# Sparse attention: the two sums of an item's output moved from VectorE to GpSimd, with both halves copied out of PSUM by ScalarE

## The chip, the cores and the metric

The kernel runs on one core of a Trainium2 chip. The metric is the device time of one execution in microseconds. Engines are named as in the profile: PE is TensorE (PEld its weight loads), DVE is VectorE, ACT is ScalarE, POOL is GpSimd, SP issues most of the DMAs. Each engine works through its own list of instructions in order; an instruction that waits holds up all that stand behind it on that engine.

## The reference

Two decoder layers over 512 tokens of width 1024. Layer 0 mixes tokens with latent attention, layer 1 with sparse attention; each layer then cross-attends into 256 memory tokens and applies a SwiGLU block, and every sub-layer is followed by a LayerNorm of the scaled residual. The part that the change touches is the sparse attention of layer 1 (16 heads of 64 in 4 groups that share a key and value head, 128 selected keys for each query):

```python
def one_block(args):                      # 128 queries at a time
    ...
    dots = jnp.einsum('bqhd,bkd->bqhk', qi_blk, k_idx) * (IDX_DIM ** -0.5)
    score = jnp.einsum('bqh,bqhk->bqk', wi_blk, jax.nn.relu(dots))
    _, sel = lax.top_k(score, topk)       # topk = 128
    k_sel, v_sel = gather_rows(k, sel), gather_rows(v, sel)
    ...
    logits = jnp.einsum('bqngd,bqknd->bqngk', qg, k_sel) * (DSA_HEAD_DIM ** -0.5)
    logits = jnp.where(sel_ok[:, :, None, None, :], logits + bias, -jnp.inf)
    p = jax.nn.softmax(logits, axis=-1)
    o = jnp.einsum('bqngk,bqknd->bqngd', p, v_sel)
...
return from_blocks(out) @ w_o
```

## The kernel before, in words

Products of float32 accuracy are made from two parts: `split` (lines 97 to 100) rounds a tile to a high part on ACT (L98) and leaves the low part, the difference, to DVE or POOL (L100); `mm3` (L121 to L123) then adds three matmuls of such parts. `chunk` loads a block of weights and splits it; some blocks of the output projection of layer 1 (`wl`, 128x1024) are split on POOL.

The sparse attention does not gather. It keeps all keys and adds a mask, and it works in 16 items, number 4*qt + g for query block qt = 0 to 3 and group g = 0 to 3. An item has three steps. `dsa_scores` makes four score tiles (L1030 adds the mask, L1031 and L1032 the products), each in a PSUM bank of the tag "b"; DVE adds the bias and takes the row's extreme (L410), and ACT takes the exponential (L416). `dsa_t` transposes the weights of qt + 1 key blocks (L1045 for qt 0 and 1, L1047 for 2 and 3) into banks of the tag "a" and splits them (L98 on ACT, L100 on DVE; for qt 0 L103, L104, L105 on ACT and PE); it also takes the reciprocal of the row sums (L420, DVE) and spreads it over a tile `rb` (L421, POOL). `dsa_pv` multiplies by the values (L1057, L1058). The value weights hold high and low parts in 128 columns, so rows 0 to 63 and 64 to 127 of the result `po` have to be added: this is the "sum" of the change, in two instructions, since heads of even and odd number go to the lower and the upper half of `OF`. Then `rb` is transposed (L1068), `OF` is multiplied by it (L1069, DVE), and `OF` is split into the operands of the output projection, for items 0 to 11 on POOL (L1073, L1074), for items 12 to 15 on ACT and DVE (L98, L100, tiles 128x128).

There are four banks of the tag "a". They are handed out in turn to the transposes, to `po` and to the transposed `rb` (`pr_`); a bank can be written again when the last reader of the tile that was in it is done. Four more are of the tag "b".

A scheduler sets the order in which the instructions of different items stand on each engine. Items 0 to 11 are run with the scores and transposes of later items between their steps (`LA = 12`); from item 12 on, the scores are all out, and matmuls of the output projection of layer 1 (L121 to L123 with `wh`, `wl`) fill in between the items. Ahead of the stage, from about 840 to 890 us, DVE selects the top keys (L964, L965); behind it, from 980 us on, comes the rest of the output projection.

Of the kernel before, what the change touches and what calls it, by code (L numbers as in the profile page):

```python
# [15 lines left out]
ALU = mybir.AluOpType  # L16
# [4 lines left out]
P = 128  # L21
# [45 lines left out]
def tile_hybrid_mla_dsa_deepnorm_block(ctx: ExitStack, tc: tile.TileContext, A: dict, out: bass.AP):  # L67
    nc = tc.nc
# [9 lines left out]
    def nm(s):  # L78
        uid[0] += 1
        return f"{s}_{uid[0]}"  # L80

    def t2(dt=F32, shape=(P, 512)):
        return tp.tile(list(shape), dt, tag="t2", name=nm("t2"), bufs=39)
# [7 lines left out]
    def bank(tag, shape=(P, 512)):  # L91
        return pp.tile(list(shape), F32, tag=tag, name=nm("ps"))
# [4 lines left out]
    def split(h, l, src, eng=None, after=None):  # L97
        nc.scalar.copy(h, src)  # L98
        with behind(after):
            (eng or nc.vector).tensor_tensor(l, src, h.bitcast(F32), op=ALU.subtract)  # L100
# [423 lines left out]
    OF = {}  # L524
# [528 lines left out]
    def dsa_pv(qt, g, rb, PT):  # L1053
        ts_ = slice(P * qt, P * qt + P)
        po = bank("a")
        for kb in range(qt + 1):
            nc.tensor.matmul(po, VD[:, kb, g], PT[kb][0], start=(kb == 0), stop=False)  # L1057
            nc.tensor.matmul(po, VD[:, kb, g], PT[kb][1], start=False, stop=(kb == qt))  # L1058
        tmp = t2()
        nc.scalar.copy(tmp[0:64], po[64:128])  # L1060
        OF = t2(F32, (P, 2, P))
        ov = po[0:64].rearrange("p (i j q) -> p i j q", j=2, q=P)
        tv = tmp[0:64].rearrange("p (i j q) -> p i j q", j=2, q=P)
        for e in range(2):
            nc.vector.tensor_tensor(OF[64 * e:64 * e + 64], ov[:, :, e], tv[:, :, e], op=ALU.add)
        pr_ = bank("a", (P, 2, P))
        for i in range(2):
            nc.tensor.transpose(pr_[:, i], rb[:, 2 * i:2 * i + 2].rearrange("p a b -> p (a b)"), ident)  # L1068
        nc.vector.tensor_tensor(OF, OF, pr_, op=ALU.mult)  # L1069
        for i in range(2):  # L1070
            oh_, ol_ = OTd[2 * g + i]
            if qt < 3:
                nc.gpsimd.tensor_copy(oh_[:, ts_], OF[:, i])  # L1073
                nc.gpsimd.tensor_tensor(ol_[:, ts_], OF[:, i], oh_[:, ts_].bitcast(F32), op=ALU.subtract)  # L1074
            else:
                split(oh_[:, ts_], ol_[:, ts_], OF[:, i])
# [17 lines left out]
    for i in range(16):  # L1094
        a = 1 if i < LA else 0
        if i != LA:
            run_s(i + 1 + a)
            run_t(i + a)
        dsa_pv(*items[i], *PT.pop(i))
        for _ in range(NTI):  # L1100
            if todo:
                topk(*todo.pop(0))
# [94 lines left out]
```

## Time and profile before

| what | value |
|---|---|
| median of 3 runs | 1549.07 us (1548.76 to 1550.13) |
| the profiled execution's own time | 1550.88 us |
| its span in the profile | 1549.1 us |
| PE busy | 1510.6 us (98%) |
| DVE busy | 996.6 us (64%) |
| ACT busy | 650.1 us (42%) |
| POOL busy | 321.8 us (21%) |

The profiled execution took 1.8 us more than its span, and 1.8 us more than the median of the runs. The shares are means over the whole kernel; the stage that the change touches lies between about 890 and 985 us. A matmul's record is longer than the distance to the next one, so a busy PE is not PE at its peak.

### The profile page before, as it was taken

The page shows a single profiled execution, that of the slowest core. Times are in us where ns is not written, and L with a number is a line of the kernel's source. Part 1 is how long each engine was busy: PE and PEld are TensorE (multiplying, and loading weights), DVE is VectorE, ACT ScalarE, POOL GpSimd, SP SyncE. Part 2 cuts the span into 40 slices and gives each one's busy share as a digit, 9 for nine tenths or more (in the row PEclk, how much of TensorE's full clock was granted, in tenths as well). Part 3 has the DMA queues.
Part 4 walks back from the last instruction along what each step waited for, and adds up shares of the span by engine and source line. Part 5 has one row for each costly group of instructions (what it writes and reads, how often), then busy time and mean ns, then how long its engine had stood idle before and what let it go on. Part 6 is the DMA issues. An engine that isn't in the chain of part 4 may idle for free.

```text
span 1549.1 us, 20803 instructions
## 1 busy us (share of the span) xinstructions
PE 1510.6 (98%) x7940; PEld 1290.5 (83%) x7940; DVE 996.6 (64%) x1709; ACT 650.1 (42%) x1150; POOL 321.8 (21%) x332
## 2 busy tenths in 40 slices
PE   9999999999999999999999899999999999999997
PEld 8788888988888888888888688898988888888886
DVE  6888868554746565654668979675548465656535
ACT  4677743343233333332246478334332333333320
POOL 2322101000132331400124553010002322324003
PEclk9999999999999999999999999999999999999999
DMA  6234424322323232223242337333323232322321
GB/s 221 71 99 110 147 82 139 120 87 91 130 88 116 75 121 86 98 90 109 83 150 69 96 109 245 109 109 110 109 90 128 78 113 94 106 94 88 96 94 55
DMA packets 51321, 166.79 MB, mean 108 GB/s; under 512 B 5300, under 2 KB 11748, under 8 KB 49172
## 3 DMA queue, kind: packets, MB, share of 16 engines
q1 hardware_dynamic: 50788, 164.41, 31.7%
q8 instruction: 62, 1.02, 0.3%
q10 hardware_dynamic: 432, 1.05, 0.2%
q14 instruction: 39, 0.32, 0.1%
HBM read 161.20 MB, written 9.47 MB: 110 GB/s over the span
## 4 chain that ended last, share of the span: by engine, by line
PE 80%; DVE 10%; ACT 3%; DMA 3%; issue 2%; POOL 1%; POOLq 0%; ACTq 0%; DVEq 0%; SPq 0%
PE ps L121 25%; PE ps L123 25%; PE ps L122 25%; DVE t L100 2%; DVE t L965 2%; DVE m L964 1%; ACT wh L98 1%; DVE wl L100 1%; ACT t L98 1%; PE ps L329 1%; PE ps L1047 1%; PE ps L1045 1%; POOL sm L272 1%; PE ps L1030 1%; ACT t L416 1%
## 5 line engine op out<-in xcount | busy, mean ns | idle before, releaser
L121 PE MATMUL ps<-t,wh 128*128 128x512 f32 (+1 forms) x1264 | 459.2, 363 | 3.4 <-DVE t L100 3.4
L122 PE MATMUL ps<-t,wh 128*128 128x512 f32 (+1 forms) x1264 | 458.1, 362 | 1.4 <-DVE t L100 1.4
L123 PE MATMUL ps<-t,wl 128*128 128x512 f32 (+1 forms) x1264 | 458.1, 362 | 0.0
L98 ACT CAST wh<-raw 128x1024 fp32r<-128x1024 f32 (+2 forms) x218 | 227.4, 1044 | 455.2 <-PE ps L122 168.2
L100 DVE TENSOR_TENSOR wl<-raw,wh 128x1024 fp32r<-128x1024 f32 (+2 forms) x197 | 253.2, 1287 | 226.7 <-ACT wh L98 224.9
L121 PE MATMUL ps<-wh,t 128*128 128x512 f32 (+2 forms) x838 | 305.0, 364 | 2.6 <-DVE t L100 1.5
L123 PE MATMUL ps<-wh,t 128*128 128x512 f32 (+2 forms) x838 | 303.1, 362 | 0.0
L122 PE MATMUL ps<-wl,t 128*128 128x512 f32 (+2 forms) x838 | 302.3, 361 | 0.0
L121 PEld LDWEIGHTS ps<-t,wh 128*128 128x128 f32 x1264 | 238.6, 189 | 41.8 <-DVE t L100 5.5
L122 PEld LDWEIGHTS ps<-t,wh 128*128 128x128 f32 x1264 | 238.6, 189 | 38.1 <-DVE t L100 1.9
L123 PEld LDWEIGHTS ps<-t,wl 128*128 128x128 f32 x1264 | 238.6, 189 | 37.2
L121 PEld LDWEIGHTS ps<-wh,t 128*128 128x128 f32 x838 | 159.0, 190 | 26.1 <-DVE t L100 1.7
L123 PEld LDWEIGHTS ps<-wh,t 128*128 128x128 f32 x838 | 158.9, 190 | 24.0 <-DVE t L100 0.5
L98 ACT CAST t<-ps 128x512 fp32r<-128x512 f32 (+2 forms) x249 | 122.9, 525 | 133.0 <-PE ps L329 87.8
L122 PEld LDWEIGHTS ps<-wl,t 128*128 128x128 f32 x838 | 159.1, 190 | 23.0
L270 POOL TENSOR_SCALAR sm<-sm 128x1 f32<-128x1 f32 x32 | 19.0, 594 | 674.7 <-DVE sm L304 634.5
L100 DVE TENSOR_TENSOR t<-ps,t 128x512 fp32r<-128x512 f32 (+2 forms) x249 | 144.1, 606 | 22.3 <-ACT t L98 20.7
L98 ACT CAST wh<-t 128x1024 fp32r<-128x1024 f32 x56 | 58.9, 1052 | 141.5 <-PE ps L122 123.5
L100 DVE TENSOR_TENSOR wl<-t,wh 128x1024 fp32r<-128x1024 f32 x56 | 71.2, 1272 | 64.8 <-ACT wh L98 63.1
L843 DVE TENSOR_TENSOR t<-ps,t 128x512 f32<-128x512 f32 x44 | 30.4, 692 | 120.4 <-PE ps L123 120.4
L100 DVE TENSOR_TENSOR t<-t,t 128x512 fp32r<-128x512 f32 (+2 forms) x113 | 83.9, 746 | 23.7 <-ACT t L98 21.5
L98 ACT CAST t<-t 128x512 fp32r<-128x512 f32 (+2 forms) x113 | 64.5, 574 | 57.7 <-POOL t L777 33.3
(177 smaller groups left out, 1690.5 us busy)
## 6 DMA issues: line engine op xcount, KB each, us to landing
raw<-in_ffn_in_dram SPq DMA_DIRECT2D x88, 512.0 KB, 3.2
t<-in_ffn_dg_dram SPq DMA_DIRECT2D x16, 1024.0 KB, 5.0
raw<-in_xa_k_dram SPq DMA_DIRECT2D x16, 512.0 KB, 3.2
raw<-in_xa_v_dram SPq DMA_DIRECT2D x16, 512.0 KB, 3.7
raw<-in_xa_q_dram SPq DMA_DIRECT2D x16, 512.0 KB, 3.7
raw<-in_xa_o_dram SPq DMA_DIRECT2D x16, 512.0 KB, 3.2
raw<-in_ffn_dl_dram SPq DMA_DIRECT2D x12, 512.0 KB, 3.2
scr<-vscr SPq DMA_DIRECT2D x16, 319.5 KB, 4.4
```

The source lines that it names most:

```text
L98: nc.scalar.copy(h, src)
L100: (eng or nc.vector).tensor_tensor(l, src, h.bitcast(F32), op=ALU.subtract)
L121: nc.tensor.matmul(ps, st[0], mv[0], start=start, stop=False, skip_group_check=more)
L122: nc.tensor.matmul(ps, st[0], mv[1], start=False, stop=False, skip_group_check=more)
L123: nc.tensor.matmul(ps, st[1], mv[0], start=False, stop=stop, skip_group_check=more)
L270: nc.gpsimd.tensor_scalar(a, var, scale, eps, op0=ALU.mult, op1=ALU.add)
L272: nc.gpsimd.tensor_tensor(b, a, mhalf, op=ALU.pow)
L329: nc.tensor.transpose(pt[:, k], x_of(tt)[:, 512 * n + P * k:512 * n + P * k + P], ident)
L416: nc.scalar.activation(Sx, src, AF.Exp, bias=nb, scale=scale, accum_out=self.sm[:, i:i + 1])
L843: nc.vector.tensor_tensor(sg, pu, sg, op=ALU.mult)
L964: nc.vector.max(out=m8, in_=acc[:, :n])
L965: nc.vector.match_replace(out=acc[:, :n], in_to_replace=m8, in_values=acc[:, :n], imm_value=-3e38)
```

## The change

The second half of `po` is no longer read by DVE straight from PSUM. ACT copies both halves of `po` to SBUF (two copies in place of one), and the two sums are made on POOL from these copies. All else of the step stays: the transposes of `rb`, the multiplication on DVE, the splits. An item uses one 128x512 buffer of the tag "t2" more.

```diff
@@ dsa_pv
-        tmp = t2()
-        nc.scalar.copy(tmp[0:64], po[64:128])
+        halves = []
+        for rows in (slice(64, 128), slice(0, 64)):
+            tmp = t2()
+            nc.scalar.copy(tmp[0:64], po[rows])
+            halves.append(tmp[0:64].rearrange("p (i j q) -> p i j q", j=2, q=P))
         OF = t2(F32, (P, 2, P))
-        ov = po[0:64].rearrange("p (i j q) -> p i j q", j=2, q=P)
-        tv = tmp[0:64].rearrange("p (i j q) -> p i j q", j=2, q=P)
         for e in range(2):
-            nc.vector.tensor_tensor(OF[64 * e:64 * e + 64], ov[:, :, e], tv[:, :, e], op=ALU.add)
+            nc.gpsimd.tensor_tensor(OF[64 * e:64 * e + 64], halves[1][:, :, e], halves[0][:, :, e], op=ALU.add)
```

In the changed kernel the copy is line 1062, the sum 1066, and each later line of `dsa_pv` has a number higher by one (the multiplication is L1070, the splits on POOL L1074 and L1075). The scheduler orders the whole stage anew. Three places of the lists follow.

First place: DVE, where the selection of the keys ends (L969) and the results of items 0 and 1 meet the scores of item 4 (L410). Before:

```order
L969 TENSOR_SCALAR t_1536_10860<-t_1462_10553 128x512
L1065 TENSOR_TENSOR t_1691_11517<-ps_11512,t_1690_11515 64x256 x2
L1069 TENSOR_TENSOR t_1691_11517<-t_1691_11517,ps_11520 128x256
L1065 TENSOR_TENSOR t_1707_11576<-ps_11571,t_1706_11574 64x256 x2
L1069 TENSOR_TENSOR t_1707_11576<-t_1707_11576,ps_11579 128x256
L410 ISA t_1710_11590,sm_11592<-ps_11594,t_1710_11590 128x256
```

The same place on DVE of the changed kernel:

```order
L969 TENSOR_SCALAR t_1536_10860<-t_1462_10553 128x512
L1070 TENSOR_TENSOR t_1692_11519<-t_1692_11519,ps_11522 128x256
L1070 TENSOR_TENSOR t_1709_11580<-t_1709_11580,ps_11583 128x256
L410 ISA t_1712_11594,sm_11596<-ps_11598,t_1712_11594 128x256
L410 ISA sm_11596 128x1
```

The four sums are gone; both multiplications, of items 0 and 1, still stand ahead of item 4's first L410.

Second place: POOL around the result of item 4 (`t_1764` is its `OF` before, `t_1769` in the changed kernel; `t_1783` and `t_1789` are item 5's). Before:

```order
L421 COPY t_1754_11749<-sm_11750 128x256
L100 TENSOR_TENSOR wl_12669<-raw_12666,wh_12668 128x1024
L421 COPY t_1773_11817<-sm_11818 128x256
L1073 CAST t_1665_11459<-t_1764_11778 128x128 x2
L1074 TENSOR_TENSOR t_1665_11459<-t_1764_11778,t_1665_11459 128x128 x2
L1073 CAST t_1666_11460<-t_1783_11846 128x128
```

The same place on POOL of the changed kernel:

```order
L421 COPY t_1758_11757<-sm_11758 128x256
L100 TENSOR_TENSOR wl_12701<-raw_12698,wh_12700 128x1024
L1066 TENSOR_TENSOR t_1769_11788<-t_1768_11786,t_1767_11784 64x256 x2
L421 COPY t_1778_11827<-sm_11828 128x256
L1074 CAST t_1665_11459<-t_1769_11788 128x128 x2
L1075 TENSOR_TENSOR t_1665_11459<-t_1769_11788,t_1665_11459 128x128 x2
L1066 TENSOR_TENSOR t_1789_11858<-t_1788_11856,t_1787_11854 64x256 x2
L421 COPY t_1798_11897<-sm_11898 128x256
L100 TENSOR_TENSOR wl_12731<-raw_12728,wh_12730 128x1024
```

Item 4's sums stand behind a split of weights (`wl`, 128x1024); a second such split stands between the sums of items 5 and 6, and a third, further on, between those of 7 and 8.

Third place: PE between the last product of item 13 and the first of item 14 (`ps_12417` and `ps_12443` are item 13's `po`; `ps_12507` and `ps_12535` item 14's; L1047 are item 14's transposes; L121 to L123 with `wh`, `wl` belong to the output projection). Before:

```order
L1058 MATMUL ps_12417<-t_1941_12414,t_1449_10402 128x512
L1047 MATMUL ps_12471<-ident,t_1921_12349 128x128 x3
L1047 MATMUL ps_12480<-ident,t_1921_12349 128x128 x4
L123 MATMUL ps_12604<-wh_12608,t_1665_11459 128x512
L121 MATMUL ps_12605<-wh_12608,t_1665_11459 128x512
L122 MATMUL ps_12605<-wl_12609,t_1665_11459 128x512
L123 MATMUL ps_12605<-wh_12608,t_1665_11459 128x512
L1047 MATMUL ps_12489<-ident,t_1921_12349 128x128 x4
L1047 MATMUL ps_12498<-ident,t_1921_12349 128x128 x4
L121 MATMUL ps_12602<-wh_12608,t_1665_11459 128x512
L1057 MATMUL ps_12507<-t_1956_12476,t_1449_10402 128x512
```

The same place on PE of the changed kernel:

```order
L1058 MATMUL ps_12443<-t_1954_12440,t_1449_10402 128x512
L1047 MATMUL ps_12499<-ident,t_1934_12375 128x128 x2
L1047 MATMUL ps_12508<-ident,t_1934_12375 128x128 x4
L123 MATMUL ps_12636<-wh_12640,t_1665_11459 128x512
L121 MATMUL ps_12637<-wh_12640,t_1665_11459 128x512
L1047 MATMUL ps_12517<-ident,t_1934_12375 128x128 x4
L122 MATMUL ps_12637<-wl_12641,t_1665_11459 128x512
L123 MATMUL ps_12637<-wh_12640,t_1665_11459 128x512
L121 MATMUL ps_12634<-wh_12640,t_1665_11459 128x512
L1047 MATMUL ps_12526<-ident,t_1934_12375 128x128 x4
L122 MATMUL ps_12634<-wl_12641,t_1665_11459 128x512
L1057 MATMUL ps_12535<-t_1970_12504,t_1449_10402 128x512
```

There are six matmuls of the output projection here instead of five, and one transpose of item 14 less; the last group of transposes has moved behind five of them.

## Rows read from the trace of the kernel before

**Rows 1.** The page, part 1: the span, and PE's busy time.
```profile
span 1549.1 us, 20803 instructions
PE 1510.6 (98%) x7940; PEld 1290.5 (83%) x7940; DVE 996.6 (64%) x1709; ACT 650.1 (42%) x1150; POOL 321.8 (21%) x332
```
**Rows 2.** Windows: stretch, length, busy us (count) of PE, PEld, DVE, ACT, POOL; clock; DMA.
```profile
905.00:915.00 10.00, 8.97 (x65) 7.99 (x66) 6.90 (x34) 8.86 (x29) 5.90 (x11) 1.00 0.19 55
...
985.00:1000.00 15.00, 15.00 (x68) 12.43 (x67) 10.53 (x15) 5.24 (x7) 0.00 (x0) 1.00 0.47 143
```
**Rows 3.** Waits, 880 to 985 us: waiter, releaser, total us, times, longest.
```profile
PE ps L1030 <- DVE sm L410: 7.8, 2, 7.4
DVE t L1065 <- ACT t L1060: 6.8, 8, 1.9
PE ps L1068 <- DVE t L1065: 1.2, 2, 0.9
...
PE ps L1068 <- DVE t L100: 0.2, 1, 0.2
```
**Rows 4.** Groups by line and shape, 880 to 985 us: busy us, mean ns.
```profile
L1065 DVE TENSOR_TENSOR t<-ps,t 64x256 f32<-64x256 f32 x32 | 13.3, 416 | 7.4 <-ACT t L1060 6.8 <-POOL wl L100 0.4
L100 POOL TENSOR_TENSOR wl<-raw,wh 128x1024 fp32r<-128x1024 f32 x5 | 12.0, 2391 | 0.0
L1074 POOL TENSOR_TENSOR t<-t,t 128x128 fp32r<-128x128 f32 x24 | 10.7, 459 | 0.5
L1060 ACT COPY t<-ps 64x512 f32<-64x512 f32 x16 | 9.3, 583 | 6.5 <-PE ps L1058 6.3
```
**Rows 5.** Lines 776 and 778 on POOL: ns min/median/max, first and last start.
```profile
L776 POOL TENSOR_TENSOR t<-t,t x16: 737/740/857, 445.0 to 1422.8; 128x256 f32<-128x256 f32 x16
L778 POOL TENSOR_TENSOR t<-t x16: 1184/1720/1728, 445.7 to 1423.5; 128x256 f32<-128x256 f32 x16
```
**Rows 6.** Timeline, items 1 and 4: start, us, engine, line, [idle before <-releaser].
```profile
903.49 0.58 ACT L1060 COPY t<-ps 64x512 f32<-64x512 f32 x1
...
904.16 0.85 DVE L1065 TENSOR_TENSOR t<-ps,t 64x256 f32<-64x256 f32 x2 [1.86 <-ACT t L1060]
905.12 0.42 DVE L1069 TENSOR_TENSOR t<-t,ps 128x256 f32<-128x256 f32 x1
...
905.45 0.42 DVE L410 CUSTOM_DVE_ANT_0 t<-ps,t 128x256 f32<-128x256 f32 x1
...
905.93 0.38 PE L1030 MATMUL ps<-t,identr 128*128 128x256 f32 x1 [0.37 <-DVE sm L410]
```
**Rows 7.** Timeline, item 4: the weight split on POOL, and item 5's first product.
```profile
919.51 2.38 POOL L100 TENSOR_TENSOR wl<-raw,wh 128x1024 fp32r<-128x1024 f32 x1
...
921.81 0.47 PE L1057 MATMUL ps<-t,t 128*128 128x512 f32 x1
```
**Rows 8.** Timeline, from item 13's last product to item 14's first.
```profile
967.62 0.48 PE L1058 MATMUL ps<-t,t 128*128 128x512 f32 x1
...
968.13 0.58 ACT L1060 COPY t<-ps 64x512 f32<-64x512 f32 x1 [1.27 <-PE ps L1058]
...
968.62 0.72 ACT L416 ACTIVATE t<-t,sm 128x512 f32<-128x512 f32 x1
...
968.75 0.85 DVE L1065 TENSOR_TENSOR t<-ps,t 64x256 f32<-64x256 f32 x2 [0.94 <-ACT t L1060]
...
969.15 0.39 PE L122 MATMUL ps<-wl,t 128*128 128x512 f32 x1
...
969.38 0.40 PE L123 MATMUL ps<-wh,t 128*128 128x512 f32 x1
...
969.72 0.39 DVE L1069 TENSOR_TENSOR t<-t,ps 128x256 f32<-128x256 f32 x1
...
970.07 1.29 DVE L100 TENSOR_TENSOR t<-ps,t 128x512 fp32r<-128x512 f32 x2
...
970.89 0.43 PE L1057 MATMUL ps<-t,t 128*128 128x512 f32 x1
```

## The prediction, made before the changed kernel had run

> **What bounds the kernel now.** I read the page first: PE is busy 1510.6 us of a span of 1549.1 us [rows 1]. The change lies in one stage of some 95 us, so I went to the windows of that stage. From 905 to 915 us PE is at 8.97 of 10 us, ACT at 8.86, DVE at 6.90 and POOL at 5.90; from 985 us on PE runs without a gap, 15.00 of 15 us, while DVE, ACT and POOL have room [rows 2]. So the stage ends when PE has worked off its list, and only what makes PE wait counts.
>
> The view of the waits says what that is. DVE stands 6.8 us in all at the sums that the change takes from it (L1065), each time because ACT's copy is late. PE itself waits little: 7.8 us at L1030 for DVE, of which one wait of 7.4 us is at the end of the key selection, ahead of the first sum; then 1.2 us and 0.2 us at L1068 [rows 3]. What a relieved DVE could still give PE is thus 7.8 - 7.4 + 1.2 + 0.2 = 1.8 us. That is the ceiling of the gain, although DVE loses 32 sums and 13.3 us of work [rows 4].
>
> **The change part by part.** DVE loses two sums of 0.416 us per item, 0.85 us as a pair [rows 4, 8]. ACT gains a copy of 0.583 us per item, 16 in all [rows 4]. A copy lets the next instruction on ACT start 0.49 us after its own start (968.13 to 968.62) [rows 8], so two copies take 0.49 + 0.58 = 1.07 us from the first start to the last end.
>
> POOL gains 32 sums. No row shows a 64x256 sum on POOL. The nearest are sums of the same 256 columns over 128 partitions: 0.740 us at the median of L776, 1.720 us at that of L778 [rows 5]; the lower end is the 0.459 us of a 128x128 difference, half the columns [rows 4]. I take 0.74 us, since L776 also reads two tiles that other engines have left long ago, while L778 shares its time with DVE's splits of SBUF tiles. A pair then takes 0.70 + 0.74 = 1.44 us, the second starting a little before the first ends, as the pair of DVE does (0.85 for two of 0.416). The two ends make a pair of 0.9 or of 3.4 us.
>
> The rule that speaks against the change: the Trainium skill's GPSIMD Engine Reference (section "Engine selection") sends an elementwise sum to VectorE, because GpSimd is about twice as slow with two inputs. Here the trace agrees: 0.740 us of L776 against DVE's 0.416 us for the same columns is a factor of 1.8. By the page's factor of two the pair would be an estimated 1.66 us and the sum below about 1 us larger.
>
> So from the first copy to the multiplication it takes 1.07 + 1.44 and two handovers of 0.05 = 2.61 us; before, 968.13 to 969.72 = 1.59 us [rows 8]. The chain of each item grows by 1.0 us. DVE now waits for POOL at the multiplication instead of for ACT at the sums, and behind that wait stand scores and splits for PE. Whether it costs anything depends on the place.
>
> *First place, items 0 and 1: +1.4 us.* In DVE's list both multiplications stand ahead of item 4's first L410, and PE's next score (L1030, 905.93) waits for that L410 (905.45) to free its bank [rows 6]. ACT's second copy for item 0 pushes item 1's copy from 903.49 to some 903.94 (0 to 0.49 us are possible; I take 0.45, as ACT's splits between the two are bound to one another). Then 1.07 of copies, 0.05, 1.44 of sums, 0.05 and the multiplication, 0.33 us ahead of L410 (905.12 to 905.45): 903.94 + 2.94 = 906.88 instead of 905.45. POOL is free in time: item 0's sums end near 902.9, and its four splits, at most 4 x 0.459 = 1.8 us [rows 4], near 905. Nothing covers this, since PE has no other row there. With sums of 0.46 us it would be +0.9, with 1.72 us +3.4.
>
> *Second place, items 4 and 6: +1.2 us.* A weight split of 2.391 us [rows 4] stands on POOL ahead of item 4's sums, where before it ran from 919.51 beside the work of the other engines and delayed only a spreading [rows 7]. Item 4's multiplication, a score and the splits of item 6's transposes on DVE, and item 5's transpose of `rb` on PE, now wait for it. Each of the two places costs between nothing (the split is over when the copies are) and 2.4 us; before, DVE and PE moved on at 921.81 [rows 7], just when that split ended, so it can be late only by little: I take 0.6 us each. The same split ahead of item 8's sums has more distance, and I put it at nothing; without that distance it costs as much as the others.
>
> *Third place, from item 12 to 13, 13 to 14 and 14 to 15: +3.0 us.* Here the chain is closed. Item 13's last product starts at 967.62; the copy follows at 968.13, the multiplication at 969.72, DVE's split of item 14's first transposes at 970.07, and item 14's first product at 970.89 [rows 8]. PE has 5 matmuls of the output projection and the transposes to fill that time, and they fill it to the tenth. In the changed kernel the chain is 1.0 us longer, and the filler is six matmuls for five but one transpose less; besides, its last transposes need the bank that the multiplication frees. A matmul is 0.23 us (969.15 to 969.38) [rows 8], so 0.8 to 1.0 us stay uncovered. The step from 14 to 15 is alike. From 12 to 13 there are six more matmuls than before (1.4 us), but item 12's sums stand on POOL behind those of item 11 and its four splits (1.44 and up to 1.8 us), and the transposes of item 13 wait for their multiplication; I take 1.2 us, between 0 and 2.9. In all 1.2 + 1.0 + 0.8 = 3.0.
>
> *The other items: -0.6 us.* For items 2, 3, 5 and 7 to 11 scores and transposes of later items stand between a product and whatever needs its bank, three us and more of PE's list; the longer chain fits in, and DVE has 0.85 us less to do per item. If this cover were gone they would cost up to 1.0 us each, 8 us. Of the ceiling of 1.8 us I take a third. Item 15's result is needed some 18 groups of three projection matmuls after its last product, 18 x 3 x 0.23 = 12 us, and costs nothing.
>
> Sum: 1.4 + 1.2 + 3.0 - 0.6 = +5.0 us. The profiled execution would go from 1550.88 to 1555.9 us; since it lies 1.8 us above the median of the runs shown, I add the difference to the median: 1549.07 + 5.0 = 1554.1 us.
>
> **The rivals.** *The relief of DVE wins.* If the scheduler's new order hides every longer chain, PE gets back the 1.8 us that it still waits for DVE: 1547.3 us, not slower. For it: DVE is near its limit in much of the stage and stood 6.8 us at L1065 [rows 3]. It decides where the sums on POOL end before DVE reaches the multiplication; at items 0 and 1 that would need a pair of sums in less than zero time, so it can only hold later on.
>
> *The waits fall where PE has other work.* The first place stays (+1.4), the third is half covered by the reordered filler (+1.5), the rest cancels: +2 to +3 us, 1551.1 to 1552.1 us. For it: the scheduler has put more matmuls of the projection between items 12 and 13. Against it: from 13 to 14 the filler is the same.
>
> *POOL is slowed by DVE.* If the sums take 1.72 us like L778 [rows 5], the pair is 2.0 us longer: 2.0 more at the first place and at each of three handovers, 4 more in the middle, 12 on top of 5.0: +17, 1566 us; with only the three handovers hit, where DVE splits the SBUF tiles of items 12 to 15, 5.0 + 6 = +11, 1560 us. The Trainium skill's page SBUF — State Buffer ("Who interferes with whom") names this: a DVE instruction with two SBUF inputs and a GpSimd instruction that reads SBUF lock each other out. The trace's L778 bears it out elsewhere; in this stage nearly all of DVE's work has one input in PSUM (t<-ps,t), as L1065 has [rows 4], which speaks against it here.
>
> **How the numbers follow.** My forecast (+3.1 to +8 us) 0.58; POOL slowed or the covered items uncovered (+8 and more) 0.14; waits covered (+0.5 to +3.1) 0.20; relief wins 0.08. A measurement of this kernel can tell about 0.2%, 3.1 us, from no change. Slower by more than that: 0.58 + 0.14 = 0.72; faster by that much is beyond the ceiling of 1.8 us and would need PE's waits to be undercounted: 0.05; the rest, 0.23, is no change. The range leaves out the relief case and the upper half of the slowed one: from +0.5 to +11 us, 1549.6 to 1560.0.
>
> **What would show it.** First step: in the changed trace DVE waits for POOL at L1070 near 905 us, and PE's L1030 behind it comes near 907.4 instead of 905.93; an L1030 at 906 would refute it. POOL's sums: a median near 0.74 us. Second: a wait at L1070 for item 4 that ends with a POOL row behind `wl`. Third: from item 13's last product to item 14's first about 4.2 us instead of 3.27. DVE's waits for ACT at the sums gone, those for POOL at L1070 larger than 6.8 us in all. Wrong I would be if DVE's list reaches L1070 late enough that POOL is done, or if POOL holds buffers that ACT and DVE want back, a wait that I have not priced.

## The result: 13 us slower, and the profile after

The changed kernel takes 1561.96 us (median of 6 runs, 1559.99 to 1563.31), the kernel before 1548.98 us (6 runs beside it). The ratio is 1.0079, with a 95% interval from 1.0068 to 1.0089: slower by 13.0 us, 0.8%. The direction is the one foretold; the size is not: +5.0 us was forecast, and 1562 us lies beyond the range. The profiled execution of the changed kernel took 1559.99 us.

On the page PE is as busy as before [rows 1], and the span is longer: what is new is idle time of PE.

```profile
span 1558.2 us, 20828 instructions
PE 1510.3 (97%) x7940; PEld 1288.8 (83%) x7940; DVE 984.7 (63%) x1677; ACT 657.3 (42%) x1166; POOL 345.1 (22%) x364
```

Windows between the same pieces of work show where (columns as in [rows 2]). They run from item 0's first product to item 4's, on to item 12's, and on to the first transposes of the next norm (L329). First before, then the changed kernel:

```profile
897.01:917.02 20.01, 17.93 (x126) 15.50 (x125) 14.50 (x57) 17.07 (x52) 9.98 (x17) 1.00 0.17 54
917.02:958.46 41.44, 40.97 (x241) 34.43 (x240) 37.97 (x111) 36.32 (x90) 21.00 (x43) 1.00 0.75 257
958.46:1006.93 48.47, 48.35 (x240) 39.68 (x239) 35.25 (x72) 21.15 (x45) 4.25 (x9) 1.00 0.39 128
```

```profile
895.71:918.48 22.77, 17.75 (x127) 15.40 (x125) 12.21 (x54) 18.01 (x55) 15.06 (x24) 1.00 0.15 48
918.48:964.73 46.25, 41.75 (x245) 34.42 (x243) 33.02 (x96) 41.80 (x105) 31.89 (x58) 1.00 0.67 231
964.73:1016.72 51.99, 48.46 (x238) 38.88 (x236) 30.07 (x57) 22.18 (x44) 11.09 (x19) 1.00 0.35 119
```

PE's idle time (length less PE's busy time) goes from 2.1 to 5.0 us, from 0.5 to 4.5 and from 0.1 to 3.5: 2.9, 4.0 and 3.4 us more, 10.4 in all. The granted clock is 1.00 in all six stretches.

The waits from 880 to 1000 us (waiter, releaser, total us, times, longest) answer to [rows 3]. L1070 is the multiplication that was L1069, L1066 the sums, L1062 the copies, L1069 now the transpose of `rb`.

```profile
DVE t L1070 <- POOL t L1066: 29.4, 16, 4.4
...
PE ps L1030 <- DVE sm L410: 9.4, 2, 7.4
...
PE ps L1047 <- DVE t L1070: 3.9, 5, 1.4
...
PE ps L1069 <- DVE t L1070: 2.3, 2, 1.5
...
PE ps L1057 <- DVE t L1070: 1.7, 2, 0.9
...
PE ps L1045 <- DVE t L1070: 1.4, 1, 1.4
```

DVE waits for POOL at all 16 multiplications, 29.4 us, where it waited 6.8 us for ACT before. That alone costs nothing. The last four rows do: PE waits 3.9 + 2.3 + 1.7 + 1.4 = 9.3 us for the multiplication itself, a releaser that [rows 3] does not have at all. The transposes L1047, L1045 and L1069 and the product L1057 write into PSUM banks that are handed out in turn. The only thing that they need of the multiplication is such a bank, one that still holds `pr_`, the transposed factor that the multiplication has yet to read. At L1030 another 9.4 - 7.4 = 2.0 us stand for DVE's queue, where before it was 0.4.

The groups by line and shape show that the operations cost what was expected of them:

```profile
L1066 POOL TENSOR_TENSOR t<-t,t 64x256 f32<-64x256 f32 x32 | 23.2, 725 | 36.7 <-ACT t L1062 35.5
L1062 ACT COPY t<-ps 64x512 f32<-64x512 f32 x32 | 18.6, 581 | 6.2 <-PE ps L1058 4.3 <-POOL t L1075 1.3
```

A sum on POOL takes 725 ns (0.74 us was taken from L776), 1.74 times DVE's 416.

**The first place.** The timeline of items 0 and 1 (start, us, engine, line, idle time and releaser):

```profile
901.82 0.42 DVE L1070 TENSOR_TENSOR t<-t,ps 128x256 f32<-128x256 f32 x1 [2.03 <-POOL t L1066]
...
902.30 0.71 PE L1045 MATMUL ps<-ident,t 128*128 128x128 f32 x4 [1.43 <-DVE t L1070]
...
902.77 0.48 PE L104 MATMUL ps<-t,identn 128*128 128x512 f32 x1
...
903.28 0.58 ACT L105 CAST t<-ps 128x512 fp32r<-128x512 f32 x1 [1.83 <-PE ps L104]
903.89 1.17 ACT L1062 COPY t<-ps 64x512 f32<-64x512 f32 x2
...
905.14 1.51 POOL L1066 TENSOR_TENSOR t<-t,t 64x256 f32<-64x256 f32 x2 [1.40 <-ACT t L1062]
...
906.68 0.42 DVE L1070 TENSOR_TENSOR t<-t,ps 128x256 f32<-128x256 f32 x1 [4.43 <-POOL t L1066]
907.02 0.42 DVE L410 CUSTOM_DVE_ANT_0 t<-ps,t 128x256 f32<-128x256 f32 x1
...
907.50 0.39 PE L1030 MATMUL ps<-t,identr 128*128 128x256 f32 x1 [1.93 <-DVE sm L410]
```

Read it downwards, as one chain. Item 0's multiplication comes late; the transposes L1045 wait 1.43 us for its bank; ACT's split L105 waits for them; item 1's two copies stand behind that split in ACT's queue; then come the sums, item 1's multiplication, L410 and, at 907.50, PE's next score. In this execution the stage had begun 1.30 us earlier than in the profile of before (first product of item 0 at 895.71 against 897.01), so the 1.57 us from 905.93 [rows 6] to 907.50 are a loss of 1.57 + 1.30 = 2.9 us.

**The second place.** Around item 4, POOL, DVE and PE:

```profile
921.72 2.35 POOL L100 TENSOR_TENSOR wl<-raw,wh 128x1024 fp32r<-128x1024 f32 x1
922.00 1.19 ACT L1062 COPY t<-ps 64x512 f32<-64x512 f32 x2
...
924.04 1.52 POOL L1066 TENSOR_TENSOR t<-t,t 64x256 f32<-64x256 f32 x2
...
925.60 0.42 DVE L1070 TENSOR_TENSOR t<-t,ps 128x256 f32<-128x256 f32 x1 [1.05 <-POOL t L1066]
...
926.16 0.41 PE L1069 MATMUL ps<-ident,t 128*128 128x128 f32 x2 [1.48 <-DVE t L1070]
```

The copies end at 923.19, the sums start only at 924.04 when the weight split is done, and item 5's transpose of `rb` waits 1.48 us.

Further on, at item 8, the third such split (941.67 to 944.07) pushes back more than the sums. It pushes the splits of item 7's result on POOL (L1074, L1075), and item 8's second copy on ACT waits for those:

```profile
945.42 0.58 ACT L1062 COPY t<-ps 64x512 f32<-64x512 f32 x1 [1.31 <-POOL t L1075]
...
946.05 0.66 PE L1047 MATMUL ps<-ident,t 128*128 128x128 f32 x4 [0.56 <-ACT t L1062]
...
948.11 0.50 PE L1057 MATMUL ps<-t,t 128*128 128x512 f32 x1 [0.94 <-DVE t L1070]
```

A copy takes nothing from POOL but the buffer of the tag "t2" that it writes to, so this is a wait for a buffer that POOL held. PE waits 0.56 + 0.94 = 1.50 us there.

**The third place.** From item 13's last product to item 14's first, which answers to [rows 8]:

```profile
975.34 0.48 PE L1058 MATMUL ps<-t,t 128*128 128x512 f32 x1
...
975.86 1.19 ACT L1062 COPY t<-ps 64x512 f32<-64x512 f32 x2 [1.80 <-PE ps L1058]
...
977.12 1.53 POOL L1066 TENSOR_TENSOR t<-t,t 64x256 f32<-64x256 f32 x2 [5.96 <-ACT t L1062]
...
978.69 0.42 DVE L1070 TENSOR_TENSOR t<-t,ps 128x256 f32<-128x256 f32 x1 [3.69 <-POOL t L1066]
979.14 0.50 ACT L98 CAST t<-t 128x128 fp32r<-128x128 f32 x2 [1.13 <-DVE t L1070]
979.16 0.66 PE L1047 MATMUL ps<-ident,t 128*128 128x128 f32 x4 [0.71 <-DVE t L1070]
...
979.90 0.39 PE L1057 MATMUL ps<-t,t 128*128 128x512 f32 x1
```

4.56 us instead of 3.27; from the first copy to the multiplication it is 2.83 us instead of 1.59. This span does not give the loss by itself, since the new order has also moved matmuls of the projection out from between item 13's products, which take 975.34 - 973.15 = 2.19 us here and 967.62 - 964.13 = 3.49 before; by PE's idle time the loss from item 12 on is the 3.4 us above. By the first transposes of the next norm (L329) PE is at 1016.72 against 1006.93 us, 9.8 us late, or 11.1 with the head start.

### The profile page after: what moved, and what is told of

The parts are those of the page before. It is cut to its first block, busy times and chain, and to the rows that moved or that the text cites. A ratio compares the mean times of both kernels' runs of the same rounds, so it can differ in the third digit from the quotient of the medians.

```text
span 1558.2 us, 20828 instructions
## 1 busy us (share of the span) xinstructions
PE 1510.3 (97%) x7940; PEld 1288.8 (83%) x7940; DVE 984.7 (63%) x1677; ACT 657.3 (42%) x1166; POOL 345.1 (22%) x364
## 4 chain that ended last, share of the span: by engine, by line
PE 77%; DVE 10%; POOL 4%; ACT 4%; issue 4%; DMA 2%; POOLq 0%; ACTq 0%; DVEq 0%
PE ps L121 25%; PE ps L123 25%; PE ps L122 24%; DVE t L100 2%; DVE t L965 2%; DVE m L964 1%; POOL t L1066 1%; ACT wh L98 1%; ACT t L98 1%; ACT t L416 1%; DVE wl L100 1%; POOL wl L100 1%; PE ps L329 1%; POOL sm L272 1%; DVE t L325 1%
## 5 line engine op out<-in xcount | busy, mean ns | idle before, releaser
L121 PE MATMUL ps<-t,wh 128*128 128x512 f32 (+1 forms) x1264 | 459.2, 363 | 3.4 <-DVE t L100 3.4
L123 PE MATMUL ps<-t,wl 128*128 128x512 f32 (+1 forms) x1264 | 458.1, 362 | 0.0
L121 PE MATMUL ps<-wh,t 128*128 128x512 f32 (+2 forms) x838 | 305.0, 364 | 2.9 <-DVE t L100 1.5
L123 PE MATMUL ps<-wh,t 128*128 128x512 f32 (+2 forms) x838 | 303.1, 362 | 0.0
L121 PEld LDWEIGHTS ps<-t,wh 128*128 128x128 f32 x1264 | 238.6, 189 | 41.9 <-DVE t L100 5.5
L123 PEld LDWEIGHTS ps<-t,wl 128*128 128x128 f32 x1264 | 238.6, 189 | 36.8
L121 PEld LDWEIGHTS ps<-wh,t 128*128 128x128 f32 x838 | 159.2, 190 | 26.6 <-DVE t L100 1.7
L123 PEld LDWEIGHTS ps<-wh,t 128*128 128x128 f32 x838 | 159.1, 190 | 23.5 <-DVE t L100 0.3
```

The costliest lines, as they stand in the source:

```text
L121: nc.tensor.matmul(ps, st[0], mv[0], start=start, stop=False, skip_group_check=more)
L123: nc.tensor.matmul(ps, st[1], mv[0], start=False, stop=stop, skip_group_check=more)
```

## The experiments

Theory: every item's longer chain (second copy, two sums on POOL) reaches PE, by the bank of `pr_` or by what stands behind the multiplication in DVE's queue. Rivals: ACT's 16 further copies; the places of the prediction alone; and something that only the whole change brings about. All medians are of timed runs, beside runs of the kernel before on the same chip.

**1. The change for four items at a time.** Four kernels, `qt` 0 to 3:

```diff
+        if qt == 0:        # 1, 2, 3 in the other three
             halves = []
             ...
                 nc.gpsimd.tensor_tensor(OF[64 * e:64 * e + 64], halves[1][:, :, e], halves[0][:, :, e], op=ALU.add)
+        else:
+            nc.scalar.copy(tmp[0:64], po[64:128])
             ...
+                nc.vector.tensor_tensor(OF[64 * e:64 * e + 64], ov[:, :, e], tv[:, :, e], op=ALU.add)
```

> The change is made for the items of query tile 0 only (items 0 to 3); the twelve others have their sums on DVE as before. Theory of places (the longer chain costs where PE's next work needs the multiplication's bank or what stands behind it in DVE's queue; read from the milestones of the two traces): +2.9 us over before, 1551.9 us; DVE waits for POOL ahead of the first key selection's score and L1030 comes near 907.4. Rival, every item alike (each pays the same for its copy and its sums): +13.0 / 4 = +3.2 us, the same in all four quarters, so that this quarter alone does not tell the two apart but the four together do. Rival, only together (POOL's or ACT's whole load makes the loss): under +1 us.

> The change for the items of query tile 1 only (items 4 to 7). Theory of places: +2.4 us over before, 1551.4 us, with PE waiting at L1069 for item 5's transpose of rb and at a score behind item 6's multiplication. Rival, every item alike: +3.2 us. Rival, only together: under +1 us.

> The change for the items of query tile 2 only (items 8 to 11). Theory of places: +1.6 us over before, 1550.6 us; the prediction on record has these at nothing or a little below (-0.3 us, 1548.7). Rival, every item alike: +3.2 us. Rival, only together: under +1 us.

> The change for the items of query tile 3 only (items 12 to 15). Theory of places: the largest quarter, +4.2 us over before, 1553.2 us, with PE waiting at the transposes L1047 of items 13, 14 and 15 for the multiplication of the item before; the prediction on record has +3.0. Rival, every item alike: +3.2 us. Rival, only together: under +1 us. If the four quarters sum to 10 to 14 us, the loss is made item by item; if they sum to less than 6 us, it needs the whole of it.

Before: 1549.39 us.

| items | us | difference of medians | ratio, 95% interval |
|---|---|---|---|
| 0 to 3 | 1552.79 | +3.4 | 1.0021 (1.0010 to 1.0032) |
| 4 to 7 | 1550.83 | +1.4 | 1.0015 (1.0006 to 1.0024) |
| 8 to 11 | 1550.80 | +1.4 | 1.0006 (0.9997 to 1.0015) |
| 12 to 15 | 1553.39 | +4.0 | 1.0026 (1.0015 to 1.0036) |

The differences add up to 10.2 us, with the places as expected: the first and the last quarter bear most, the middle ones the rest. (The ratios are not formed from the medians; that of items 4 to 7 stands for 2.3 us and that of 8 to 11 for 0.9. The four ratios together stand for 10.5 us, that of the whole change for 12.2.) That speaks against "only together". Against "every item alike" it speaks less firmly: the intervals of the third and the fourth quarter just touch, at 1.0015. The quarter of items 8 to 11 is not told from nothing by itself. 2.8 us of the 13.0 are in no quarter; the four intervals together leave about 3 us open, so this alone proves nothing, and the next run asks after it.

**2. All items but the first four.**

```diff
-        if qt == 0:
+        if qt > 0:
```

> The change for items 4 to 15, items 0 to 3 as before. The four quarters taken singly measured +3.4, +1.4, +1.4 and +4.0 us, 10.2 in all, against 13.0 of the whole change: 2.8 us belong to no quarter. Theory 1 (they are made in items 0 to 3 when PE's stall there is long enough that the granted clock falls to 0.50 again for some 3 us, as the profiles of the kernel with its sums on DVE, of the one with the copied factor and of the one with the weight splits on DVE show near 908 to 911 us): without items 0 to 3 the rest adds up, +6.9 us over before, 1556.3 us, and no stretch at 0.50 after 900. Theory 2 (the later quarters get in each other's way): +9 to +10 us, 1559 us.

1556.31 us, +7.0 (ratio 1.0047, 1.0034 to 1.0061): where Theory 1 put it (that it fits to the tenth is luck), and the other wanted +9 to +10. The interval, +5.3 to +9.5 us, just reaches that. The profile speaks for Theory 1 too: the granted clock is 1.00 from 900 us to the end of the stage. The windows from 900 to 910 us, of the kernel with items 0 to 3 alone and then of this one, show where PE's idle time goes with the first quarter (8.40 us busy before, 5.83 in the changed kernel):

```profile
900.00:910.00 10.00, 5.83 (x39) 4.58 (x38) 3.53 (x19) 5.72 (x18) 6.96 (x15) 1.00 0.13 47
```

```profile
900.00:910.00 10.00, 8.38 (x57) 7.05 (x58) 6.64 (x30) 7.35 (x21) 5.49 (x10) 1.00 0.04 17
```

**3. The changed kernel once more, for its clock.** No edit.

> The changed kernel once more, for a second profile beside its time. The first profiled execution had the time 1559.99 us and a mean granted clock of 0.997, the other five runs 1561.3 to 1563.3 us and 0.993 to 0.994. Theory 1 (the clock falls again after PE's stalls at items 0 and 1 in most executions, and this makes 2 to 3 us): a profiled run at 0.994 shows a stretch at 0.50 between 905 and 913 us that the first one lacks; one at 0.997 shows none. Rival (the difference lies before 900, in how late the clock comes back after the key selection): no such stretch, but a later return near 895 us.

1563.78 us, +14.5 (1.0090, 1.0075 to 1.0106). The profiled execution (1563.46 us, mean granted clock 0.993) has what the first one (0.997) lacks. The same window, first of this execution, then of the first:

```profile
907.50:915.50 8.00, 7.25 (x38) 7.16 (x38) 4.48 (x23) 4.68 (x14) 4.11 (x6) 0.57 0.01 2
```

```profile
907.50:915.50 8.00, 7.15 (x52) 6.50 (x53) 5.12 (x27) 7.81 (x26) 6.06 (x10) 1.00 0.19 57
```

PE is as busy, but 38 pieces of work stand in place of 52: the granted clock is down at 1.2 GHz for most of the stretch. Ahead of it PE had waited 1.43 us for the multiplication, 0.51 us without a releaser that the profile shows, and 1.93 us for DVE, which are the same waits as in the first execution. The price can be read from one product to another: from L1057 of item 2 to that of item 3 it takes 915.68 - 904.66 = 11.02 us here and 912.52 - 903.92 = 8.60 there, 2.4 us more. The rival has a part too: before 900 the clock came back 2 us later here, worth 0.7 us (904.66 against 903.92). The Trainium skill's page TensorE: Matmul & The Clock Gate ("HAM oscillation — how this bites in real kernels") says that waits between pieces of PE's work can drop its clock, so that the next piece begins cold. Its case is one of waits for DMA; this trace agrees that the clock falls after waits, here for other engines and none above 1.93 us, at a price of 2.4 us, and the first profile shows that the same waits do not always do it.

The profiles show what is left without such a fall. From item 0's first product to the next norm's first transposes it takes 109.92 us before and 121.01 in the first execution of the changed kernel, 11.1 more (in the second, with its fall, 123.58). In the profiles of experiment 1 it takes 113.00, 111.58, 111.88 and 113.93 us, that is 3.08, 1.66, 1.96 and 4.01 more, 10.7 in all; none of these has a fall in it. So the parts do add up but for 0.4 us, and what the medians have beyond them goes with the clock. That it falls in most executions of the whole change is inferred from the times: the first execution is 11.0 us above the median of before, the five others, at 0.993 to 0.994, are 12.4 to 14.3 us above. Why it falls so often there stays open, since the profile of items 0 to 3 alone shows the same waits of 1.43, 0.51 and 1.93 us and no fall.

**4. ACT or POOL?** Both halves copied by ACT, the sums on DVE:

```diff
-            nc.gpsimd.tensor_tensor(OF[64 * e:64 * e + 64], halves[1][:, :, e], halves[0][:, :, e], op=ALU.add)
+            nc.vector.tensor_tensor(OF[64 * e:64 * e + 64], halves[1][:, :, e], halves[0][:, :, e], op=ALU.add)
```

> As after, both halves copied by ACT, but the two sums of each item stay on DVE, out of SBUF tiles. Theory (the sums on POOL, 1.5 us a pair, and what waits behind them, are the loss): the chain grows by the second copy alone, 0.5 us an item, and DVE's pair is no longer than before: +1 to +4 us over before, 1550 to 1553 us. Rival, ACT (its 16 further copies push its splits and exponentials back): +10 to +13 us, near after's 1562.

1554.06 us, +4.6 (1.0025, 1.0016 to 1.0034), a little above the +1 to +4 expected. ACT is not the bulk: some 8.4 of the 13.0 us go when the sums leave POOL. The second copy is not free either. Runs with a mean clock of 0.996 took 1550.1 to 1551.2 us, those with 0.994 took 1553.5 to 1555.1, which suggests that part of the +4.6 is the clock again. The profile (1554.07 us) has a granted clock of 0.53 from 906 to 908 us and 0.62 in the two after; from item 0's first product to the next norm PE is idle there for 5.4 us in place of 2.7, so waits remain as well. Its waits have none of PE for the multiplication beyond 0.7 us:

```profile
PE ps L1030 <- DVE sm L410: 8.8, 2, 7.4
...
DVE t L1066 <- ACT t L1062: 8.4, 6, 2.7
...
PE ps L1045 <- DVE t L1070: 0.7, 1, 0.7
```

**5. The price of the chain.** POOL's second sum of each item is done twice, with the same result:

```diff
-        for e in range(2):
+        for e in (0, 1, 1):
```

> As after, with the second sum of each item done twice on POOL (same result), which makes the chain from the product to the multiplication 0.74 us longer in all 16 items and changes nothing on ACT, DVE or PE. Theory of the chain (after the change nearly every item's chain is on the path to PE: the chains of 16 items are 16.4 us longer in all and the time 13.0 us, 0.8 of a us for each): 16 x 0.74 x 0.8 = +9.5 us over after, 1571.5 us. Rival, the places of the prediction (chain exposed at two items at the start and three handovers at the end): 5 x 0.74 = +3.7 us, 1565.7. Rival, POOL is fast enough once PE waits anyway: under +2 us.

1572.59 us (1.0148, 1.0132 to 1.0163), 10.6 us above the changed kernel's first median and 8.8 above the one sent with it. 16 sums of 0.73 us are 11.7 us, so that three quarters or more of every further microsecond reach PE. The rivals (3.7 us, or under 2) fall. The clock is hardly the difference: in this profile it is down for about 7 us, from 910 to 914 us and again from 982 to 986, and in that of the run sent with it for as long, from 908 to 915. The further sum also holds up what stands behind it in POOL's list, the spreading of `rb` and the splits; this run doesn't tell the two apart. The waits have the same rows as after, and larger:

```profile
DVE t L1070 <- POOL t L1066: 38.2, 14, 6.0
...
PE ps L1047 <- DVE t L1070: 6.2, 4, 2.6
PE ps L1069 <- DVE t L1070: 5.9, 4, 2.8
```

**6. Bank or queue?** ACT copies the factor out of PSUM, so that its bank is free without POOL; the multiplication stays on DVE:

```diff
-        nc.vector.tensor_tensor(OF, OF, pr_, op=ALU.mult)
+        rbt = t2(F32, (P, 2, P))
+        nc.scalar.copy(rbt, pr_)
+        nc.vector.tensor_tensor(OF, OF, rbt, op=ALU.mult)
```

> As after, but ACT also copies the transposed factor out of its PSUM bank, and the multiplication on DVE reads that copy, so that the bank is free without POOL. Theory A (PE waits for the bank that the multiplication frees): most of PE's waits at L1047, L1057 and L1069 go, and the time falls to 1552 to 1556 us; DVE still waits for POOL, and what stands behind it in DVE's queue still comes late. Theory B (what stands behind the waiting multiplication in DVE's queue is what PE lacks): the time stays at 1559 to 1563 us. Theory C (ACT's load): 16 further copies make it worse, 1564 us or more.

1559.39 us, +9.9 (1.0067, 1.0054 to 1.0081): within Theory B, so the reading of the waits as waits for banks is too simple. Freeing the bank gives 2.6 us against the first median (4.4 against the second), with the price of 16 further copies on ACT in it; what stands behind the multiplication (L1072 here) in DVE's queue still comes late. PE has no wait for L1072 itself, as Theory A had said, but others have taken its place, among them 1.9 us at the transposes of `rb` that end with POOL rows (L1077). L1030 at item 4 waits as it did, 1.94 us for 1.93:

```profile
DVE t L1072 <- POOL t L1066: 26.5, 13, 4.1
...
PE ps L1030 <- DVE sm L410: 10.4, 4, 7.4
...
PE ps L1057 <- DVE t L100: 2.8, 3, 1.5
```

The Trainium skill's page PSUM — Partial Sum Buffer ("Engine vs sequencer instructions") calls the queues of ScalarE, VectorE and GpSimdE strict first in, first out; this run agrees: with no bank to be freed by the multiplication, L410 still came only after it, at 907.01 behind 906.67.

**7. The multiplication on POOL as well**, so that DVE waits for POOL nowhere ahead of the result's own splits:

```diff
-        nc.vector.tensor_tensor(OF, OF, rbt, op=ALU.mult)
+        nc.gpsimd.tensor_tensor(OF, OF, rbt, op=ALU.mult)
```

> As the kernel with the factor copied by ACT, but the multiplication on POOL too, so that DVE waits for POOL nowhere in an item's output before the splits of its result, and no PSUM bank waits for POOL. Theory (the loss is the wait for POOL, by bank and by queue): 1547 to 1552 us, about before. Rival, ACT's load: still 1558 us or more. Rival, POOL's results come too late for the output projection: a wait at the first rows of the projection that need them, with the loss at the end of the stage.

1557.93 us, +8.5 (1.0058, 1.0044 to 1.0072): the expectation of 1547 to 1552 fell. Item 13's first product is 2.9 us late against the start of item 0 (10.3 in the changed kernel), so most of the loss up to there is gone; it has moved to the end, to items 13 to 15. There the result is split by ACT and DVE, and now ACT stands where DVE stood:

```profile
966.36 0.72 POOL L1072 TENSOR_TENSOR t<-t,t 128x256 f32<-128x256 f32 x1
967.11 0.50 ACT L98 CAST t<-t 128x128 fp32r<-128x128 f32 x2 [2.89 <-POOL t L1072]
...
967.52 0.58 ACT L98 CAST t<-ps 128x512 fp32r<-128x512 f32 x1
...
968.15 0.50 PE L1057 MATMUL ps<-t,t 128*128 128x512 f32 x1 [2.32 <-ACT t L98]
```

The split of item 13's next transposes (967.52, out of PSUM) stands in ACT's list behind a wait of 2.89 us for POOL's product, and PE waits 2.32 us for it. The clock fell here as well: 0.83 from 970 to 980 us. The loss lies at the end of the stage, as the third rival had it, but not at the rows of the projection.

**8. The weight splits away from POOL.** The splits of the output projection, five of them in the stage, on DVE:

```diff
-            return chunk(w(n, c), (P, 2, 512), nc.gpsimd if pin[1] else None, pin)
+            return chunk(w(n, c), (P, 2, 512), None, pin)
```

> As after, but the six weight splits of the output projection that stand on POOL among the sums (2.4 us each) go to DVE. Theory (the prediction's second place: item 4's and item 6's sums wait behind such a split): 1 to 2.5 us under after, 1559.5 to 1561 us, with DVE's waits at L1070 of these items shorter. Rival, DVE's queue (a split of some 1 us or more on DVE delays what PE waits for): the same as after or up to 4 us above it.

1559.11 us, +9.6 over before (1.0064, 1.0051 to 1.0078), 2.9 us under the changed kernel's first median, a little more than the 1 to 2.5 expected. DVE's waits at L1070 are 22.9 us for 29.4, PE's for L1070 4.1 + 1.4 + 1.0 + 0.3 = 6.8 for 9.3. This counts all five splits, not only the two that the prediction priced; the wait of ACT's copy for a buffer at item 8 is gone too.

**9. A shorter chain in the kernel before.** ACT's copy in two, each ahead of its sum:

```diff
-        nc.scalar.copy(tmp[0:64], po[64:128])
...
         for e in range(2):
+            nc.scalar.copy(tv[:, :, e], uv[:, :, e])
             nc.vector.tensor_tensor(OF[64 * e:64 * e + 64], ov[:, :, e], tv[:, :, e], op=ALU.add)
```

> The opposite direction: the kernel before, sums on DVE out of PSUM, but ACT's one copy of 64x512 is made as two of 64x256, each just ahead of the sum that needs it, so that the first sum starts some 0.2 us earlier and the chain is some 0.2 us shorter in every item; ACT has 16 more instructions. Theory of the chain, if it is as exposed in before as in after: 16 x 0.2 x 0.8 = -2.6 us, 1546.8 us. If in before only the three handovers at the end are exposed (as the prediction had it): 3 x 0.2 = -0.6 us, not to be told from before. Rival, ACT's extra instructions cost more than the chain gains: +1 us or more.

1552.36 us, +3.0 (1.0020, 1.0011 to 1.0029). It did not test what it was made for, since the chain came out longer, at items 0, 1, 13, 14 and 15 by 0.2 to 2.0 us: at item 13 an exponential stands between the two copies, and from the first copy to the multiplication it takes 971.77 - 969.18 = 2.59 us for 1.59 [rows 8].

```profile
969.18 0.37 ACT L1065 COPY t<-ps 64x256 f32<-64x256 f32 x1 [1.24 <-PE ps L1058]
969.45 0.72 ACT L416 ACTIVATE t<-t,sm 128x512 f32<-128x512 f32 x1
...
970.17 0.36 ACT L1065 COPY t<-ps 64x256 f32<-64x256 f32 x1
```

Whether a shorter chain would gain stays open. No version here beats the kernel before.

## Why the prediction had the direction and not the size

**The operations and the handover were right.** POOL's pair takes 1.51 to 1.53 us (forecast 1.44), the chain from copy to multiplication 2.83 (2.61), item 13's last product to item 14's first 4.56 us (4.2). DVE's waits for POOL exceed 6.8 us. The rival of POOL slowed by DVE did not come about: the sums stand at 725 ns, not at the 1.72 us of L778. No gain from the relief of DVE is to be seen: it stands 29.4 us at the multiplication.

**What failed is the cover.** "The longer chain fits in" was said of items 2, 3, 5 and 7 to 11, and "I put it at nothing" of item 8's sums; neither held. The prediction had priced lost cover at up to 8 us and gave everything of +8 and more a chance of 0.14; this is the case that came, and the range left its upper half out. By places, with the loss by the runs of experiment 1 and by PE's idle time in the first profile (which has no fall of the clock):

| items | forecast | runs | idle time of PE |
|---|---|---|---|
| 0 to 3 | +1.4 | +3.4 | +2.9 |
| 4 to 11 | +1.2 - 0.6 = +0.6 | +2.8 | +4.0 |
| 12 to 15 | +3.0 | +4.0 | +3.4 |

**First place.** The wrong term is "item 1's copy at some 903.94", 0.45 us late. It started at 903.89 in a stage that began 1.30 us earlier, so it was 1.7 us late; that L1030 stands at 907.50, near the 907.4 that I had named, is an accident of that head start. The step that I had not seen is the transposes L1045, which need the bank of item 0's factor; they made the split late behind which the copy waits. That the bank is only one of two ways is shown by experiment 6. There item 1's copy comes at 903.86 although the stage began 0.87 us later than in the changed kernel, so the transposes' wait for the bank was worth about 0.9 of the 2.9 us. Item 3's transposes of `rb` add a wait of 0.83 us for item 2's multiplication, one of the items that were called covered.

**Second place and the other items.** The two places that the prediction named cost more than the 0.6 us taken for each: PE waits 1.48 us behind item 4's multiplication and 0.78 behind item 6's (at item 7's first product). Nearly as much again lies where nothing was expected: 1.50 us at item 8, where the third weight split makes POOL late with its own splits and ACT's copy waits for a buffer, and 0.56 behind item 10's multiplication. The wait for a buffer is the one that the prediction's last sentence called not priced; it came in the whole change and in experiment 2. A relieved DVE does not help, since in its queue the multiplication stands ahead of the rest.

**Third place.** Right in kind and near in size. PE's idle time grows by 1.7, 0.9 and 0.8 us at the three handovers, for 1.2, 1.0 and 0.8.

**Not in the sum at all: the clock.** In the executions in which it falls after PE's stall at items 0 and 1 it costs 2.4 us (experiment 3). The prediction has no term and no rival for it.

Together 3.4 + 2.8 + 4.0 = 10.2 by the runs, 10.4 by PE's idle time, for a forecast of 5.0; the rest of the 13.0 us of the medians is put down to the clock, by inference from the times (experiment 3).

## What to carry to other kernels

Moving a small operation to a slower, idle engine costs its added latency, not its busy time, wherever a busy engine's queue has the consumer in it: here three quarters or more of an added microsecond (experiment 5). Before calling an item covered, list what its consumer releases (the PSUM bank that it reads, the buffers that the slower engine holds longer, and every row behind it in its own queue) and ask when the bottleneck engine next wants each. If the bottleneck is TensorE, add the chance that a new stall lowers its clock for the work behind it; here waits of 1.43, 0.51 and 1.93 us did so in one execution.

## What the runs showed of the hardware

The same three waits of PE (1.43, 0.51 and 1.93 us within 7 us) were followed in one execution by some 7 us at 1.2 GHz, which cost 2.4 us, and in another by none: the clock stayed at 2.4 GHz. In the profile of the kernel with items 0 to 3 alone it stayed there too, behind the same three waits. In the profiles of experiments 4, 6 and 8 a fall near the same place lasted about half as long. A stall of this kind thus has no fixed price, and runs of one kernel spread by more than those of the kernel before: 1550.1 to 1555.1 us with the sums on DVE, 1547.5 to 1551.0 before, on the same chip.
